# Layer 1's values and decay inputs: one set of columns in three passes of 348, 346 and 346, in place of four pieces of 512 columns and a product of its own

## The chip, the cores and the metric

The kernel runs on one core of one Trainium2 chip. The metric is the device time of one execution, in microseconds. Runs of the same kernel were repeated, and the median is given with the lowest and the highest.

## The reference

A decoder of two layers with 256 tokens and a width of 1024, in float32. Each layer has a token mixer and a gated feed-forward part with a short convolution; each of these is preceded by an RMS norm whose shift, scale and gate come from a conditioning vector (`ada`). Layer 0 mixes tokens by windowed attention. Layer 1, where the change lies, is gated linear attention with 4 heads in chunks of 64 tokens (keys of 128, values of 256 columns a head):

```python
proj = h @ w_in          # columns: q 512, k 512, v 1024, glr 16, r 1024
gk = log_sigmoid(glr @ w_gate + b_gate) / 16
# by head and chunk of 64 tokens
bcum = cumsum(gk);  blast = bcum[..., -1:, :]
q_t = q * 128**-0.5 * exp(bcum)
k_t = k * exp(-bcum)
k_d = k * exp(blast - bcum)
A = where(causal, q_t @ k_t.T, 0)
o = A @ v + q_t @ state          # state: state * exp(blast) + k_d.T @ v, chunk by chunk
# o is normed by head, gated with silu(r), and multiplied by w_out
```

The 16 columns `glr` are the input of the decay: `w_gate` is 16 x 512.

## The kernel before

Activations lie with the width on the 128 partitions (8 tiles `h[kt]`) and the 256 tokens in the columns. TensorE multiplies in float32r; to keep float32's precision, each activation and each weight is split into a high part, rounded to float32r, and a low part, the difference. A product is then three matmuls (`mm3`, lines 199 to 201): high by high, low by high, high by low. For a weight tile the load goes through SyncE's queue into `raw`, ScalarE casts it to `whi` (line 172) and VectorE subtracts to get `wlo` (line 178), each in two halves: that is `split`.

The program's instructions are ordered by a planner that estimates times while the kernel is built, with orders written by hand on top: `with behind(x)` puts what follows behind `x` on its engine without a wait of its own. `next_ada` loads 1 MB of the next conditioning weights and lets VectorE form their dot products with the conditioning vector (line 140); ScalarE turns them into `mod` (line 148).

Layer 1's mixer goes through these steps:

- Values `pv` are token-major. The stationary side of the matmul is a tile of `h` for 128 tokens, the moving side 512 of the 1024 value columns. Four loads of 1 MB (two tiles `kt` each) serve 2 x 2 x 2 products each, so 32 products, 96 matmuls of 512 columns, in four banks.
- After the second of the four, the decay: `log_gates` loads `w_glr` (120 KB), computes `glr` (16 rows by 256 tokens, 24 matmuls of 256 columns), VectorE copies it (line 1052), and `gates_of` forms `z` = `w_gate`'s 128 columns of a head by `glr`, one plain float32 product of inner size 16 for each head (line 1063).
- The gates are formed for head 0 (256 columns) and for heads 1 to 3 together (768 columns): on ScalarE `nz` = -z - b, then `ea` three times (absolute value, exponential, logarithm); on VectorE `sp`, the running sum `cs` (line 1075), `dl` (line 1079); on ScalarE the exponentials `e_d`, `e_q`, `e_k`, `dec`.
- `v` is copied out of the four banks, by ScalarE and VectorE.
- `states(hd)` for the four heads: `q` and `k` in the bank `pqk` (q of head 0 is there early), then on VectorE `k_d`, `q_t`, `k_t` (lines 1133 to 1135); TensorE turns `k_d` (`kdt`, line 1141), forms `a` (line 1152) and the state increments `kv` (line 1163); the states `st` follow on ScalarE and VectorE. `products(hd)` forms the head's output `o`, `normed_output` its norm. `gate(n)` computes `r` in the bank `pr`.
- The heads are called in the order states 0, states 1, output 0, states 2, products 1, states 3, normed output 1, products 2, gate 0 and so on. TensorE's queue fills the gaps between a head's small products with the next head's `pqk`.

Of the kernel before, what the change touches and what calls it, by code (L numbers as in the profile page):

```python
# [11 lines left out]
F32 = mybir.dt.float32  # L12
EXP_LN = "natural_log_exp_and_others"
F32R = mybir.dt.float32r
# [4 lines left out]
P = 128  # L19
# [11 lines left out]
NEG = -1e30  # L31
CONFIGS = ((128, 1), (512, 4), (2048, 16))
N_BUCKETS = 32
MAX_DISTANCE = 2048
ROWS = ((0, 512), (2, 128), (1, 128))
NROW = 768
# [21 lines left out]
def trunk(ctx: ExitStack, tc: tile.TileContext, I, out):  # L58
# [13 lines left out]
    def bank(name="ps", tag=None):  # L72
        tag = tag or next(cycle)
        return psum.tile([P, 512], F32, tag=tag, name=name, bufs={"p": 2, "s": 3, "t": 3}[tag])
# [76 lines left out]
        mod[l, piece, kt] = m  # L151
        return i, j

    def ada_chunk(l, n):
        raw = ada_load(l, n)
        for s in range(2):
            ada_dot(l, n, s, raw)


    last_load, copied, last_lo = [None], [None], [None]  # L160

    def split(src, n, dmas=1, after=((), ()), late=(), low=(), lows=True):
# [5 lines left out]
        lo = wspl.tile([P, 2048], F32R, tag="wlo", name="wlo")  # L168
        for i in range(0, n, n // 2):
            c = slice(i, i + n // 2)  # L170
            with behind(*after[i > 0]):
                copied[0] = nc.scalar.copy(hi[:, c], raw[:, c])  # L172
        if not lows:
            return hi, lo, raw, n // 2
        for i in range(0, n, n // 2):
            c = slice(i, i + n // 2)
            with behind(*(late if i else low)):
                last_lo[0] = nc.vector.tensor_tensor(lo[:, c], raw[:, c], hi[:, c].bitcast(F32), op=ALU.subtract)  # L178
        return hi, lo

    def low_part(w, i):
# [14 lines left out]
    def mm3(ps, a, b, start, stop):  # L196


        mm(ps, a[0], b[0], start=start, stop=False)  # L199
        mm(ps, a[0], b[1], start=False, stop=False)  # L200
        return mm(ps, a[1], b[0], start=False, stop=stop)  # L201
# [252 lines left out]
    shift(att, 8)  # L454
    rounds, first_loads = [0], []

    def next_ada():
        if rest:
            ada_chunk(*rest.pop(0))

    def next_half(after):
        l, n = rest[0]
# [556 lines left out]
    def gt(shape, name, dt=F32, bufs=1, tag=None):  # L1019
        return gla.tile(shape, dt, tag=tag or name, name=name, bufs=bufs)  # L1020
# [21 lines left out]

    glr_copy = []
# [11 lines left out]
    def gates_of(first, n, glr):  # L1055
        def new(name, tag, columns=n * T):
            return gt([P, columns], name, tag=f"{tag}{min(first, 1)}")

        nz = new("nz", "A")
        for i in range(n):  # L1060
            hd = first + i
            ps = bank("z", "sttt"[hd])
            mm(ps[:, :T], w_g[:, P * hd : P * hd + P], glr, start=True, stop=True)
            nc.scalar.activation(nz[:, T * i : T * i + T], ps[:, :T], AF.Identity,
                                 scale=-1.0, bias=nbg[:, hd : hd + 1])

        ea = new("ea", "B")
        nc.scalar.activation(ea, nz, AF.Abs)
# [3 lines left out]
        nc.vector.scalar_tensor_tensor(sp, nz, 0.0, ea, op0=ALU.max, op1=ALU.add)  # L1072

        cs = new("cs", "cs")
        nc.vector.tensor_tensor_scan(cs, keep[:, : n * T], sp, 0.0, op0=ALU.mult, op1=ALU.add)
        cs3 = cs.rearrange("p (n c) -> p n c", c=CH)
        last = cs3[:, :, CH - 1 : CH]
        dl = new("dl", "C")
        nc.vector.tensor_tensor(dl.rearrange("p (n c) -> p n c", c=CH), cs3,
                                last.to_broadcast([P, 4 * n, CH]), op=ALU.subtract)  # L1080
        e_d, e_q, e_k = (new(name, t) for name, t in (("e_d", "D"), ("e_q", "A"), ("e_k", "B")))
        nc.scalar.activation(e_d, dl, AF.Exp, scale=1.0 / 16)
        nc.scalar.activation(e_q, cs, AF.Exp, scale=-1.0 / 16)
        nc.scalar.activation(e_k, cs, AF.Exp, scale=1.0 / 16)
        dec = new("dec", "dec", 4 * n)
        nc.scalar.activation(dec, last.rearrange("p n c -> p (n c)"), AF.Exp, scale=-1.0 / 16)
        return e_q, e_k, e_d, dec

    pv = [[bank("pv", tg) for _ in range(2)] for tg in "ps"]
    for n in range(4):  # L1090
        with behind(*((), chain[5], chain[7], glr_copy)[n]):
            w = split(I["w_v_b"][n], 2048) if n else w_first
            if n > 1:
                next_ada()
        if n == 0:
            with behind(*chain[7]):
                whole(early_q)
        for i in range(2):
            kt = 2 * n + i
            for t in range(2):  # L1100
                ht = [y[:, P * t : P * t + P] for y in h[kt]]
                for s in range(2):
                    mm3(pv[t][s], ht, parts(w, D * i + 512 * s, 512), kt == 0, kt == KT - 1)
        if n == 1:
            gates = log_gates()
    v = [gt([P, D], f"v{t}") for t in range(2)]
    for t in range(2):
        nc.scalar.copy(v[t][:, 0:512], pv[t][0])
        nc.vector.tensor_copy(v[t][:, 512:D], pv[t][1])

    o_n = []
    last_a, last_sq, copies, kept = [None], [None], [None], [None, None]

    def states(hd):
# [23 lines left out]
        kd = gt([P, T], "kdT", bufs=2)  # L1138
        for t in range(2):
            c = slice(P * t, P * t + P)  # L1140
            nc.tensor.transpose(ps[:, c], k_d[:, c], ident)
        nc.scalar.copy(kd, ps[:, :T])

        a_t = gt([P, 2, P], "a_t", bufs=2)
# [11 lines left out]
            masked()  # L1156
        vh = slice(T * hd, T * hd + T)
        st = []
        kv = bank("kv", "t")
        for n in range(3):  # L1160
            t, r = n // 2, slice(CH * (n % 2), CH * (n % 2) + CH)
            d = (kv[:, :T], ps[:, T:], kv[:, T:])[n]
            last = mm(d, kd[r, P * t : P * t + P], v[t][r, vh], start=True, stop=True)
        if hd == 3:
            masked(last)
        for n in range(3):
# [12 lines left out]
    def output(hd, *state):  # L1179
        normed_output(hd, products(hd, *state))  # L1180

    def products(hd, q_t, a_t, st):
        po = bank("o", "s")
        for et in range(2):
            ev = slice(T * hd + P * et, T * hd + P * et + P)
            for t in range(2):
                d = po[:, T * et + P * t : T * et + P * t + P]
                mm(d, v[t][:, ev], a_t[:, t, :], start=True, stop=False)
                for n in range(2 * t, 2 * t + 2):
                    if n:  # L1190
                        last_o[0] = mm(po[:, T * et + CH * n : T * et + CH * n + CH],
                           st[n - 1][:, P * et : P * et + P], q_t[:, CH * n : CH * n + CH],
                           start=False, stop=(n % 2 == 1))
        return po

    def normed_output(hd, po, after=()):
# [99 lines left out]
def _laid_out(a):  # L1296
# [50 lines left out]
    A["w_v_b"] = wb[:, 1024:2048].reshape(4, 2, P, D).transpose(0, 2, 1, 3).reshape(4, P, 2 * D)  # L1347
    A["w_glr"] = wb[:, 2048:2064].reshape(KT, P, 16).transpose(1, 0, 2).reshape(P, KT * 16)
    A["w_glr"] = np.pad(A["w_glr"], ((0, 0), (0, P - 16)))
    A["w_r_b"] = pairs(wb[:, 2064:])  # L1350
    A["w_gate"] = a["w_gate_b"][0]
# [27 lines left out]
```

## Time and profile before

| | |
|---|---|
| median of 3 runs | 765.97 us (765.29 to 766.35) |
| the profiled execution's own time | 764.38 us |
| its span in the profile | 762.6 us |
| TensorE busy, share of the last chain | 754.2 us (99%), 94% |
| VectorE busy | 649.4 us (85%) |
| ScalarE busy | 486.2 us (64%) |
| granted TensorE clock | 1.000 |
| values, first to last product | 463.34 to 490.36 us |
| head 0's transposes start | 499.06 us |
| first product of the gate | 526.33 us |

The times of the rows are starts in the profiled execution. Its own time of 764.38 us holds 1.8 us that lie around the span, and is 1.6 us below the median of the runs.

### The profile page before, as it was taken

What the parts mean: (1) busy time and instruction counts of PE and PEld (TensorE: products, weight loads), DVE (VectorE), ACT (ScalarE), POOL (GpSimd) and SP (SyncE); (2) the same over time, 40 slices, a digit from 0 to 9 for tenths busy, and PEclk for the clock granted to TensorE, in tenths of its full rate; (3) what the DMA queues carried; (4) which work ended last, traced back from release to release, by engine and by line L of the source; (5) the groups of instructions that cost most, each with busy time, mean ns of one, the idle gap of its engine ahead of it and who ended that gap; (6) DMA issues with size and microseconds to landing.
All of it is one profiled execution on the core that took longest, in us unless ns stands there. A gap on an engine that the chain in (4) does not pass through costs nothing.

```text
span 762.6 us, 16024 instructions
## 1 busy us (share of the span) xinstructions
PE 754.2 (99%) x6394; PEld 731.5 (96%) x6394; DVE 649.4 (85%) x1185; ACT 486.2 (64%) x951; POOL 33.6 (4%) x56
## 2 busy tenths in 40 slices
PE   8999999999999999999999999999999999999997
PEld 6999999999999999999999998899999999999997
DVE  6997999898989678999999778797668999998592
ACT  6476676565566478776777456746766866666551
POOL 0001101101101010000000000000010000000100
PEclk9999999999999999999999999999999999999999
DMA  9988889778787357878556976875356777774631
GB/s 348 404 287 312 318 293 325 281 256 307 285 275 254 112 198 257 319 262 277 202 172 234 340 263 228 305 275 178 132 190 216 241 269 271 209 174 157 200 104 56
DMA packets 39225, 186.57 MB, mean 245 GB/s; under 512 B 9004, under 2 KB 11820, under 8 KB 25070
## 3 DMA queue, kind: packets, MB, share of 16 engines
q1 hardware_dynamic: 38768, 185.10, 69.6%
q8 instruction: 50, 0.82, 0.4%
q10 hardware_dynamic: 382, 0.45, 0.2%
q14 instruction: 25, 0.20, 0.1%
HBM read 184.43 MB, written 1.10 MB: 243 GB/s over the span
## 4 chain that ended last, share of the span: by engine, by line
PE 94%; DVE 3%; DMA 2%; issue 1%; ACT 0%; DVEq 0%; ACTq 0%
PE pab L199 10%; PE pab L200 10%; PE pab L201 10%; PE pqk L199 5%; PE pd L199 5%; PE pd L200 5%; PE pd L201 5%; PE pqk L201 5%; PE pqk L200 5%; PE pv L199 3%; PE pv L200 3%; PE pv L201 3%; PE pqk L675 2%; PE py L199 2%; PE py L201 2%; PE py L200 2%
## 5 line engine op out<-in xcount | busy, mean ns | idle before, releaser
L172 ACT CAST whi<-raw 128x1024 fp32r<-128x1024 f32 (+4 forms) x262 | 237.7, 951 | 92.6 <-PE pab L200 35.5
L178 DVE TENSOR_TENSOR wlo<-raw,whi 128x1024 fp32r<-128x1024 f32 (+3 forms) x246 | 263.8, 1097 | 38.5 <-ACT whi L172 37.5
L200 PE MATMUL pab<-hlo,whi 128*128 128x256 f32 x672 | 184.6, 276 | 0.0
L201 PE MATMUL pab<-hhi,wlo 128*128 128x256 f32 x672 | 184.6, 276 | 0.0
L199 PE MATMUL pab<-hhi,whi 128*128 128x256 f32 x672 | 183.2, 277 | 0.0
L200 PEld LDWEIGHTS pab<-hlo,whi 128*128 128x128 f32 x672 | 126.0, 188 | 0.2
L201 PEld LDWEIGHTS pab<-hhi,wlo 128*128 128x128 f32 x672 | 126.1, 188 | 0.0
L199 PEld LDWEIGHTS pab<-hhi,whi 128*128 128x128 f32 x672 | 125.1, 188 | 0.1
L140 DVE CUSTOM_DVE_ANT_0 ada_raw<-ada_raw,c_bc 128x1024 f32<-128x1024 f32 x96 | 114.1, 1229 | 4.7 <-DMA ada_raw<-in_w_ada 4.7
L199 PE MATMUL pqk<-hhi,whi 128*128 128x256 f32 x356 | 98.0, 281 | 0.0
L200 PE MATMUL pqk<-hlo,whi 128*128 128x256 f32 x356 | 97.4, 279 | 0.0
L201 PE MATMUL pqk<-hhi,wlo 128*128 128x256 f32 x356 | 96.8, 279 | 0.2 <-DVE wlo L178 0.2
L200 PE MATMUL pd<-glo,whi 128*128 128x256 f32 x308 | 84.8, 276 | 0.0
L201 PE MATMUL pd<-ghi,wlo 128*128 128x256 f32 x308 | 84.8, 276 | 0.0
L199 PE MATMUL pd<-ghi,whi 128*128 128x256 f32 x308 | 84.7, 276 | 0.0
L201 PEld LDWEIGHTS pqk<-hhi,wlo 128*128 128x128 f32 x356 | 65.9, 188 | 1.1 <-issue 0.7
L200 PEld LDWEIGHTS pqk<-hlo,whi 128*128 128x128 f32 x356 | 66.7, 188 | 0.1
L199 PEld LDWEIGHTS pqk<-hhi,whi 128*128 128x128 f32 x356 | 66.5, 188 | 0.1
L200 PEld LDWEIGHTS pd<-glo,whi 128*128 128x128 f32 x308 | 57.7, 188 | 0.0
L201 PEld LDWEIGHTS pd<-ghi,wlo 128*128 128x128 f32 x308 | 57.7, 188 | 0.0
L199 PEld LDWEIGHTS pd<-ghi,whi 128*128 128x128 f32 x308 | 57.7, 188 | 0.0
L962 ACT ACTIVATE r<-pab,small 128x256 f32<-128x256 f32 x86 | 47.5, 561 | 7.0 <-DVE r L965 6.7
(269 smaller groups left out, 1498.8 us busy)
## 6 DMA issues: line engine op xcount, KB each, us to landing
raw<-in_w_up SPq DMA_DIRECT2D x42, 1024.0 KB, 4.9
ada_raw<-in_w_ada SPq DMA_DIRECT2D x29, 1024.0 KB, 5.8
raw<-in_w_down SPq DMA_DIRECT2D x28, 704.0 KB, 4.3
ada_raw<-in_w_ada SPq DMA_DIRECT2D x38, 512.0 KB, 6.8
raw<-in_wqk SPq DMA_DIRECT2D x18, 1024.0 KB, 6.9
raw<-in_wv SPq DMA_DIRECT2D x14, 768.0 KB, 6.5
raw<-in_w SPq DMA_DIRECT2D x7, 960.0 KB, 6.5
raw<-in_w_out_a SPq DMA_DIRECT2D x4, 1024.0 KB, 6.9
```

The costliest lines, as they stand in the source:

```text
L140: i = nc.vector.tensor_tensor_reduce(w, w, c_bc, op0=ALU.mult, op1=ALU.add, scale=1.0, scalar=0.0, accum_out=dot,)
L172: copied[0] = nc.scalar.copy(hi[:, c], raw[:, c])
L178: last_lo[0] = nc.vector.tensor_tensor(lo[:, c], raw[:, c], hi[:, c].bitcast(F32), op=ALU.subtract)
L199: mm(ps, a[0], b[0], start=start, stop=False)
L200: mm(ps, a[0], b[1], start=False, stop=False)
L201: return mm(ps, a[1], b[0], start=False, stop=stop)
L675: mm(pqk[i], w[a], h[kt][b], start=s and i % 2 == 0 and (a, b) == (0, 0), stop=e and i % 2 == 1 and b == 1)
L962: nc.scalar.activation(r, u[:, :T], AF.Identity, scale=cw[2], bias=col(C_CB + 44 * l + f))
```

## The change

The 16 decay inputs become columns of the same product as the values: 16 + 1024 = 1040 columns, in three passes of 348, 346 and 346. The first pass holds the 16 and value columns 0 to 331, the others 346 value columns each. The weights lie in memory padded to 384 columns a pass and tile, in six loads of 768 KB (pass by half of the tiles `kt`), which `split` casts and subtracts through a view of the used columns. A pass uses two banks, one for each half of the tokens, so that there are 144 matmuls of 348 or 346 columns. The passes' halves are ordered: pass 0 first half, pass 1 first half, pass 0 second half, pass 1 second half, pass 2.

The decay inputs thus come out with the tokens on the partitions. `stack_parts` splits them there into a high and a low part and lays high, low and high again at columns 0, 32 and 64 of a zeroed 128 x 128 tile for each half of the tokens (six small VectorE instructions). `turn_parts` turns the two tiles with two transposes into one bank, and VectorE copies it as `glr`, now 128 x 256 float32r. `w_gate` lies in memory as 128 x 512 with its 16 rows at 0, 32 and 64; ScalarE casts it and VectorE puts the low part at rows 64 to 79. So one float32r product of inner size 128 a head gives high by high, low by high and high by low at once. The transposes come after the first two of the four tiles of pass 1's second half, z after its last.

Besides, `next_ada` takes an order, and for head 3 `products(1)` is formed before head 3's state increments, its second half behind head 3's transposes.

```diff
-        w_first = split(I["w_v_b"][0], 2048, late=last_x[1:])
+        w_first = [columns(0, 0, late=last_x[:1]), columns(1, 0, low=last_x[1:], late=last_x[1:])]
...
+    def columns(n, half, **order):
+        c = (348, 346, 346)[n]
+        return split(I["w_v_b"][n, half], 4 * 384, view=lambda w: w.rearrange("p (k c) -> p k c", k=2)[:, :, 0:c], **order)
...
-    w_g = gt([16, 512], "w_g")
-    nc.sync.dma_start(w_g, I["w_gate"])
+    w_g = gt([P, 512], "w_g", F32R)
+    w_raw = gt([P, 512], "w_raw", tag="C1")
+    nc.sync.dma_start(w_raw, I["w_gate"])
+    with behind(*chain[7]):
+        nc.scalar.copy(w_g, w_raw)
+        own = slice(STACKED[2], STACKED[2] + 16)
+        nc.vector.tensor_tensor(w_g[own, :], w_raw[own, :], w_g[own, :].bitcast(F32), op=ALU.subtract)
+    stacked = gt([P, 2, P], "stacked", F32R)
+    nc.gpsimd.memset(stacked.bitcast(F32), 0.0)
...
+    def stack_parts(pv):
+        for t in range(2):
+            hi, lo, again = (stacked[:, t, at : at + 16] for at in STACKED)
+            ps = pv[t][:, 0:16]
+            nc.vector.tensor_copy(hi, ps)
+            nc.vector.tensor_tensor(lo, ps, hi.bitcast(F32), op=ALU.subtract)
+            nc.vector.tensor_copy(again, hi.bitcast(F32))
+
+    def turn_parts():
+        ps = bank("glr", "t")
+        for t in range(2):
+            last = nc.tensor.transpose(ps[:, P * t : P * t + P], stacked[:, t, :].bitcast(F32), ident)
+        low_rank.append(nc.vector.tensor_copy(glr, ps[:, 0:T]))
+        return last
 
     def log_gates():
-        with behind(*chain[5]):
-            w_gl = split(I["w_glr"], 7 * 16 + P)
-        ps = bank("glr", "t")
-        for kt in range(KT):
-            mm3(ps[:, :T], parts(w_gl, 16 * kt), h[kt], kt == 0, kt == KT - 1)
-        glr = gt([16, T], "glr")
-        glr_copy.append(nc.vector.tensor_copy(glr, ps[:16, :T]))
-        return [gates_of(*part, glr) for part in PARTS]
+        for tg in "st":
+            ps = bank("z", tg)
+            for i in range(2):
+                hd = len(sums_of)
+                sums_of.append(ps[:, T * i : T * i + T])
+                last = mm(sums_of[hd], w_g[:, P * hd : P * hd + P], glr, start=True, stop=True)
+        return last
...
-    for n in range(4):
-        with behind(*((), chain[5], chain[7], glr_copy)[n]):
-            w = split(I["w_v_b"][n], 2048) if n else w_first
-            if n > 1:
-                next_ada()
...
+    def values(n, half, w, kts=range(4), after=()):
+        c = (348, 346, 346)[n]
+        for j in kts:
+            kt = 4 * half + j
+            with behind(*after):
+                for t in range(2):
+                    ht = [y[:, P * t : P * t + P] for y in h[kt]]
+                    last = mm3(pv[n][t][:, 0:c], ht, parts(w, 384 * j, c), kt == 0, kt == KT - 1)
+        return last
...
+    values(0, 0, w_first[0])
+    last = values(1, 0, w_first[1])
+    with behind(*chain[3]):
+        w = columns(0, 1)
+    last = values(0, 1, w, after=[last])
+    with behind(*chain[7]):
+        whole(early_q)
+    stack_parts(pv[0])
+    with behind(*chain[7]):
+        w = columns(1, 1)
+        next_ada(last_lo[0])
+    last = values(1, 1, w, range(2), [last])
+    with behind(last):
+        last = turn_parts()
+    keep_values(0)
+    last = values(1, 1, w, range(2, 4), [last])
+    with behind(last):
+        last = log_gates()
+    pv.append([bank("pv", "t") for _ in range(2)])
+    gates = [gates_of(*part) for part in PARTS]
+    with behind(*low_rank):
+        w = columns(2, 0)
+        next_ada(last_lo[0])
+    keep_values(1)
+    last = values(2, 0, w, after=[last])
+    w = columns(2, 1)
+    values(2, 1, w, after=[last])
+    keep_values(2)
...
-    po1 = products(1, *s1)
-    s3 = states(3)
-    normed_output(1, po1, last_a)
+    po1 = []
+
+    def ahead(turned):
+        po1.append(products(1, *s1, last=turned))
+        return last_o
+
+    s3 = states(3, ahead)
+    normed_output(1, po1[0], last_a)
```

More of the change, by code (lines that the diff above doesn't have):

```diff
@@ L152, in ada_dot, with ada_chunk, split @@
         return i, j
-    def ada_chunk(l, n):
+    def ada_chunk(l, n, *after):
         raw = ada_load(l, n)
-        for s in range(2):
-            ada_dot(l, n, s, raw)
+        with behind(*after):
+            for s in range(2):
+                ada_dot(l, n, s, raw)
     last_load, copied, last_lo = [None], [None], [None]
-    def split(src, n, dmas=1, after=((), ()), late=(), low=(), lows=True):
+    def split(src, n, dmas=1, after=((), ()), late=(), low=(), lows=True, view=None):
         raw = wraw.tile([P, 2048], F32, tag="raw", name="raw")
@@ L168, in split @@
         lo = wspl.tile([P, 2048], F32R, tag="wlo", name="wlo")
+        part = view or (lambda w: w)
         for i in range(0, n, n // 2):
@@ L171, in split @@
             with behind(*after[i > 0]):
-                copied[0] = nc.scalar.copy(hi[:, c], raw[:, c])
+                copied[0] = nc.scalar.copy(part(hi[:, c]), part(raw[:, c]))
         if not lows:
@@ L177, in split @@
             with behind(*(late if i else low)):
-                last_lo[0] = nc.vector.tensor_tensor(lo[:, c], raw[:, c], hi[:, c].bitcast(F32), op=ALU.subtract)
+                last_lo[0] = nc.vector.tensor_tensor(part(lo[:, c]), part(raw[:, c]), part(hi[:, c].bitcast(F32)), op=ALU.subtract)
         return hi, lo
@@ L455, in trunk, with next_ada @@
     rounds, first_loads = [0], []
-    def next_ada():
+    def next_ada(*after):
         if rest:
-            ada_chunk(*rest.pop(0))
+            ada_chunk(*rest.pop(0), *after)
     def next_half(after):
@@ L1089, in trunk @@
     pv = [[bank("pv", tg) for _ in range(2)] for tg in "ps"]
-    for n in range(4):
-        with behind(*((), chain[5], chain[7], glr_copy)[n]):
-            w = split(I["w_v_b"][n], 2048) if n else w_first
-            if n > 1:
-                next_ada()
[L1095 to L1105, printed above, removed]
@@ L1106, in trunk @@
-    v = [gt([P, D], f"v{t}") for t in range(2)]
-    for t in range(2):
-        nc.scalar.copy(v[t][:, 0:512], pv[t][0])
-        nc.vector.tensor_copy(v[t][:, 512:D], pv[t][1])
+    v = [gt([P, D], f"v{t}") for t in range(2)]
+    def values(n, half, w, kts=range(4), after=()):
+        c = (348, 346, 346)[n]
+        for j in kts:
+            kt = 4 * half + j
+            with behind(*after):
+                for t in range(2):
+                    ht = [y[:, P * t : P * t + P] for y in h[kt]]
+                    last = mm3(pv[n][t][:, 0:c], ht, parts(w, 384 * j, c), kt == 0, kt == KT - 1)
+        return last
@@ new lines, in keep_values @@
+    def keep_values(n):
+        first, c = VCUTS[n]
+        at = 0 if n else 16
+        for t, copy in enumerate((nc.scalar.copy, nc.vector.tensor_copy)):
+            copy(v[t][:, first : first + c], pv[n][t][:, at : at + c])
+    values(0, 0, w_first[0])
[9 more added lines that the diff above has]
+        next_ada(last_lo[0])
@@ L1111, in trunk, with states @@
+    keep_values(2)
     o_n = []
     last_a, last_sq, copies, kept = [None], [None], [None], [None, None]
-    def states(hd):
+    def states(hd, between=lambda turned: ()):
         if hd == 0:
@@ L1140, in states @@
             c = slice(P * t, P * t + P)
-            nc.tensor.transpose(ps[:, c], k_d[:, c], ident)
+            last_kd = nc.tensor.transpose(ps[:, c], k_d[:, c], ident)
         nc.scalar.copy(kd, ps[:, :T])
@@ L1158, in states @@
         st = []
+        ahead = between(last_kd)
         kv = bank("kv", "t")
@@ L1162, in states @@
             d = (kv[:, :T], ps[:, T:], kv[:, T:])[n]
-            last = mm(d, kd[r, P * t : P * t + P], v[t][r, vh], start=True, stop=True)
+            with behind(*ahead):
+                last = mm(d, kd[r, P * t : P * t + P], v[t][r, vh], start=True, stop=True)
         if hd == 3:
@@ L1180, in output, with products @@
         normed_output(hd, products(hd, *state))
-    def products(hd, q_t, a_t, st):
+    def products(hd, q_t, a_t, st, last=None):
         po = bank("o", "s")
@@ L1185, in products @@
             ev = slice(T * hd + P * et, T * hd + P * et + P)
[L1186 to L1193, printed above, removed]
+            with behind(*([last] if last and et else [])):
+                for t in range(2):
+                    d = po[:, T * et + P * t : T * et + P * t + P]
+                    mm(d, v[t][:, ev], a_t[:, t, :], start=True, stop=False)
+                    for n in range(2 * t, 2 * t + 2):
+                        if n:
+                            last_o[0] = mm(po[:, T * et + CH * n : T * et + CH * n + CH],
+                               st[n - 1][:, P * et : P * et + P], q_t[:, CH * n : CH * n + CH],
+                               start=False, stop=(n % 2 == 1))
         return po
```

24 lines of the change are left out of this document (15 added, 9 removed).

## The prediction, on record before the changed kernel ran

> **What bounds the kernel now.** I read the page's list of engines and the chain that ended last first, then the stretches of layer 1's mixer.
>
> ```profile
> PE 754.2 (99%) x6394; PEld 731.5 (96%) x6394; DVE 649.4 (85%) x1185; ACT 486.2 (64%) x951; POOL 33.6 (4%) x56
> PE 94%; DVE 3%; DMA 2%; issue 1%; ACT 0%; DVEq 0%; ACTq 0%
> ```
> ```profile
> core 0: us, PE busy (x) PEld busy (x) DVE busy (x) ACT busy (x) POOL busy (x), PEclk, DMA share, GB/s
> 464.00:482.00 18.00, 18.00 (x91) 15.25 (x90) 16.41 (x29) 11.62 (x24) 0.00 (x0) 1.00 0.78 300
> 485.00:499.00 14.00, 14.00 (x98) 12.96 (x97) 12.20 (x16) 13.01 (x22) 0.00 (x0) 1.00 0.68 239
> 526.00:562.00 36.00, 36.00 (x316) 35.89 (x315) 24.75 (x40) 25.34 (x42) 0.00 (x0) 1.00 0.51 176
> 757.00:760.00 3.00, 0.32 (x3) 0.08 (x1) 1.30 (x4) 1.19 (x3) 0.00 (x0) 1.00 0.10 38
> 760.00:762.60 2.60, 0.00 (x0) 0.00 (x0) 0.00 (x0) 0.00 (x0) 0.00 (x0) 0.90 0.41 158
> ```
>
> TensorE works 99% of the span and is 94% of the last chain. In the stage that is changed (464 to 499) it never stops, and after it, from 526 to 562, it is busy 36.00 us of 36.00. So a microsecond of TensorE work taken out here reaches the end, unless TensorE then comes to something that isn't ready. VectorE and ScalarE are the candidates: from 485 to 499 they are busy 12.20 and 13.01 of 14.00 us.
>
> **TensorE's work, part by part.** Matmuls are pipelined, so I price them by the distance of their starts.
>
> ```profile
> 463.34 0.59 PE L199 MATMUL pv<-whi,hhi 128*128 128x512 f32 x1
> 474.85 0.28 PE L201 MATMUL glr<-hhi,wlo 128*128 128x256 f32 x1
> 477.32 0.28 PE L201 MATMUL glr<-hhi,wlo 128*128 128x256 f32 x1
> 482.26 0.40 PE L199 MATMUL pv<-whi,hhi 128*128 128x512 f32 x1
> 484.85 0.40 PE L201 MATMUL pv<-whi,hlo 128*128 128x512 f32 x1
> 490.36 0.39 PE L201 MATMUL pv<-whi,hlo 128*128 128x512 f32 x1
> 499.06 0.38 PE L1141 MATMUL kdt<-ident,k_d 128*128 128x128 f32 x2
> 505.77 0.28 PE L201 MATMUL pqk<-hhi,wlo 128*128 128x256 f32 x1
> 506.22 0.60 PE L1152 MATMUL a<-q_t,k_t 128*128 128x128 f32 x4
> ```
>
> From 484.85 to the values' last product at 490.36 lie 8 further products of three passes each, 24 steps: 0.2294 us for 512 columns. The third and the last of glr's 24 products are 2.47 us apart, 21 steps: 0.1177 for 256 columns. Straight between the two, 346 columns take 0.1177 + 90 x 0.000436 = 0.157 (by the 512 row's price per column 0.155, by the 256 row's 0.159).
> - Values and decay inputs: 96 x 0.2294 = 22.02 becomes 144 x 0.157 = 22.61: **+0.6** (+0.3 to +0.9).
> - glr's 24 own products go: 24 x 0.1177 = **-2.82**.
> - z: from 482.26 to 484.85 there are 2.59 us, which hold two value steps and z's four products of K=16, eight passes: 2.59 - 2 x 0.2294 = **-2.13**. The four float32r products that take their place, as wide as glr's: 4 x 0.1177 = **+0.47**.
> - Two transposes of the stacked parts, 128x128 in float32 like head 1's between 505.77 and 506.22: 0.45 less two float32r steps, **+0.2**.
>
> The sum is -3.68: TensorE would come to head 0's transposes (`kdt`, 499.06 before) at 495.4.
>
> **Is k_d of head 0 there by then?** The transposes wait for VectorE's k_d, and the other heads' products stand behind them on TensorE. Rows of the two engines on the way:
>
> ```profile
> 483.32 0.91 ACT L1064 ACTIVATE nz<-z,nbg 128x256 f32<-128x256 f32 x2 [0.29 <-PE z L1063]
> 484.13 0.41 ACT L1068 ACTIVATE ea<-nz 128x256 f32<-128x256 f32 x1
> 485.45 2.00 ACT L172 CAST whi<-raw 128x1024 fp32r<-128x1024 f32 x2
> 487.34 0.85 ACT L1068 ACTIVATE ea<-nz 128x768 f32<-128x768 f32 x1
> ```
> ```profile
> 486.54 2.36 DVE L178 TENSOR_TENSOR wlo<-raw,whi 128x1024 fp32r<-128x1024 f32 x2 [2.72 <-ACT whi L172]
> 488.81 0.42 DVE L1072 SCALAR_TENSOR_TENSOR sp<-nz,ea 128x256 f32<-128x256 f32 x1
> 489.41 0.69 DVE L1109 COPY v<-pv 128x512 f32<-128x512 f32 x1 [0.17 <-PE pv L201]
> 490.01 0.68 DVE L1075 TENSOR_TENSOR_SCAN cs<-keep,sp 128x256 f32<-128x256 f32 x1
> 491.72 0.95 DVE L1072 SCALAR_TENSOR_TENSOR sp<-nz,ea 128x768 f32<-128x768 f32 x1
> 492.59 1.22 DVE L178 TENSOR_TENSOR wlo<-raw,whi 128x1024 fp32r<-128x1024 f32 x1
> 493.73 1.75 DVE L1075 TENSOR_TENSOR_SCAN cs<-keep,sp 128x768 f32<-128x768 f32 x1
> 495.39 1.20 DVE L178 TENSOR_TENSOR wlo<-raw,whi 128x1024 fp32r<-128x1024 f32 x1
> 496.51 0.42 DVE L1134 SCALAR_TENSOR_TENSOR q_t<-early_q,e_q 128x256 f32<-128x256 f32 x1
> 496.85 0.42 DVE L1133 TENSOR_TENSOR k_d<-pqk,e_d 128x256 f32<-128x256 f32 x1
> 497.51 0.95 DVE L1079 TENSOR_TENSOR dl<-cs 128x768 f32<-128x768 f32 x1
> ```
>
> Before, k_d ended at 497.27, 1.8 us ahead of its use. The order of instructions of the changed build puts, between z and k_d:
> - z ends after 96 of the 144 value products: 463.34 + 96 x 0.157 + 0.2 = 478.6; with the product's own latency (rows of 0.28 to 0.39) and four steps of 0.12, `nz` starts at about 479.1. If casts of the last pass still stand ahead on ScalarE, 480.
> - ScalarE then runs four `nz` (0.81 for two, 483.32 to 484.13: 1.6), two `ea` of 256 and two of 768 columns (a step is the duration less some 0.1 of overlap: 2 x 0.31 + 2 x 0.75), two small `mod` and a small copy (an estimate of 0.6), and the first half of head 1's weight cast (1.0). That is 5.3 us: 484.4 (to 485.4). All of these stand ahead of that cast, which before went in at 485.45, behind three of the `nz` and two `ea`.
> - VectorE waits for that cast, then runs: two halves of `wlo` 2.27; sp of head 0 0.34; half of `v` of pass 1 0.43 (between 0.60 for 512 columns and 0.33 for 256); sp of the other heads 0.87; cs 0.60; `wlo` 1.14; their cs 1.66; `wlo` 1.12; dl 0.33 (as k_d's kind); two `wlo` 2.27; their dl 0.87; q_t 0.34; k_d 0.42. Sum 12.66. Against before, two more `wlo` halves (2.3) and the wide dl (0.9), which stood behind k_d at 497.51, now stand ahead of it.
>
> So k_d ends at 497.1 to 498.1 and the transposes start 0.2 later; I take 497.8. TensorE, there at 495.4, stands idle for some 2.4 us (2.0 to 2.9), where before it had no wait. Of the 3.7 us, **1.2** are left (0.8 to 1.7).
>
> **Behind that.** `products(1)` goes ahead of head 3's state products, its second half behind head 3's transposes. That is no work more or less, but one more place where TensorE turns from float32r to float32 products between head 0's transposes and the gate (nine for eight). Between 505.77 and 506.22 three steps and two transposes are already 0.2 over the float32r pace; a turn costs 0.1 to 0.2. VectorE, late now, can also hold back head 1's k_d by some tenths. I take **+0.5** for both (+0.2 to +0.9; below nothing too, to -0.2, if a wait inside head 3 is covered by the moved products).
>
> Edits that I cost at nothing: the loads are six of 768 KB where four of 1 MB and 120 KB went, +0.4 MB, with the DMA share at 0.78 and TensorE never waiting for a load in this stretch; the cover is the pass ahead, and it is gone if a load comes over 4 us later. The strided form of the split (two runs of 346) is bounded by these rows, the second with a strided output, to 0.02 us each, twelve in all on each engine:
>
> ```profile
> L621 DVE COPY v<-pv x7: 405/409/409, 69.2 to 248.4; 64x256 f32<-64x256 f32 x7
> L622 DVE COPY v<-pv x7: 427/428/428, 69.6 to 248.8; 64x256 f32<-64x256 f32 x7
> ```
>
> The six 16-column copies that stack the parts have no row; they lie between a tiny instruction and a k_d (0.1 to 0.42 each, 0.6 to 2.5 in all) and run while twelve value products of pass 1 (1.9 us) cover them.
>
> **Sum:** -3.68 + 2.4 (the wait) + 0.5 = **-0.7** us, with -1.3 to +0.9 for the ends. The profiled execution of before took 764.38 us, 1.6 below the median of the runs, 765.97; set against the median the forecast is **765.3** (this case's own range 764.7 to 766.9). About 0.2%, 1.5 us, is what a measurement of this kernel can tell from no change.
>
> **Rivals.**
> 1. *The gain is kept.* k_d is there when TensorE comes. For it: VectorE stood idle 2.72 us ahead of 486.54, so it has room that a better meeting with ScalarE's casts could use; and the durations I sum are from a stretch with both engines full. Against it: the order is fixed, and 12.66 us behind a cast that ends at 484.4 leave over 2 us to find. The whole gain is -3.7 + 0.5 = -3.2, 762.8; half of the wait gone gives -1.9, 764.1.
> 2. *TensorE's clock drops in the new wait (slower).* It decides if a wait of 2.0 to 2.9 us is long enough. Price: at the kernel's start, after an idle 2.24 us, float32 products of 512 columns took 0.94 each, later ones 0.52:
>
> ```profile
> 2.24 3.75 PE L123 MATMUL cb<-c_row,ones_d 1*128 1x512 f32 x4 [2.24 <-DMA c_row<-in_c]
> 11.26 1.03 PE L405 MATMUL rows<-oh,tab 33*16 33x512 f32 x2
> ```
>
>    So 3.75 us or more at about half speed: at least 1.9 us lost, up to 3.5 if it lasts twice as long; -0.7 + 1.9 = +1.2 to +2.8, middle 768.0. Against it: at the end of the span TensorE did almost nothing from 757.00 on and the clock is still 1.00 up to 760, so an idle of nearly 3 us left it whole. [...]
> 3. *The stacked copies come late (slower).* They stand behind two `ada` dots and two weight subtracts on VectorE:
>
> ```profile
> L140 DVE CUSTOM_DVE_ANT_0 ada_raw<-ada_raw,c_bc 128x1024 f32<-128x1024 f32 x96 | 114.1, 1229 | 4.7 <-DMA ada_raw<-in_w_ada 4.7
> 463.72 0.33 SPq L133 DMA_DIRECT2D ada_raw<-in_w_ada  x1
> ada_raw<-in_w_ada SPq DMA_DIRECT2D x29, 1024.0 KB, 5.8
> ```
>
>    An `ada` load issued at 463.72 lands at about 469.5, and the dots have to start by about 472, since pass 0 is complete after 72 value products (474.7) and its turned parts are due after 84 (476.5). If the load slips by more than 2.5 us, the two dots (2.46) fall between pass 0's end and the copies; transposes, z, ScalarE's chain and k_d all come later by up to 2.4: +1.7, 767.7. Against it: 4.7 us in 96 dots is all that dots waited for their loads in the whole span.
>
> **How the numbers follow.** The forecast 0.45 (765.3), the gain kept wholly or by more than half 0.35 (the sum on VectorE carries the verdict, and it hangs on where two full engines meet), the clock 0.10 (768.0), the late copies 0.10 (767.7). Faster by over 0.2% needs below 764.4: rival 1 nearly whole, with a little of the forecast's lower end, 0.36. Slower needs over 767.5: rivals 2 and 3 and nothing of the forecast, 0.19 with a little of both falling inside. The rest is 0.45. The range reaches to the kept gain's far end, 762.8, but for its last part, and to the slower cases' middle: 762.9 to 767.9.
>
> **What would show it.** Right: TensorE idle for 2 to 3 us ahead of head 0's `kdt`, released by VectorE's k_d; `kdt` at 497 to 498.5; value steps of 0.155 to 0.159; the granted clock 1.00 throughout. Rival 1: no such idle, `kdt` near 495.5. Rival 2: idle and then products of twice the step. Rival 3: TensorE idle ahead of the transposes into `glr`, or z after 480. The forecast is wrong at its root if the value products take over 0.165 each, or if idle time appears after 526.

## The result, and the profile after

The changed kernel takes 766.38 us (median of 22 runs, 765.16 to 769.34), the kernel before 765.03 us (22 runs, 763.92 to 766.35). The ratio is 1.0021, 95% interval 1.0013 to 1.0029: slower by 0.21%, where 0.7 us less was forecast. The profiled execution took 768.63 us, 2.3 above its kernel's median; before, it was 1.6 below what was then the median. Two page lines of the changed kernel, busy time by engine and the last chain, and then its span with the mean granted clock:

```profile
PE 755.3 (98%) x6416; PEld 736.3 (96%) x6416; DVE 651.0 (85%) x1195; ACT 486.5 (63%) x955; POOL 33.0 (4%) x57
PE 90%; DVE 5%; DMA 2%; ACT 2%; issue 1%; DVEq 0%; ACTq 0%
```
```profile
core 0: 766.8 us, clock 0.996
```

TensorE's part of the last chain fell from 94% to 90%, VectorE's rose from 3% to 5%, ScalarE's from 0 to 2%. The mean granted clock was 1.000 before. So something made TensorE wait, and something took its clock. Its list of waits (total us, times, longest us), which before had none over 0.3 us behind the kernel's start:

```profile
PE cb L125 <- DMA c_row<-in_c: 3.0, 1, 3.0
PE kdt L1195 <- DVE k_d L1187: 3.0, 1, 3.0
```

The place in time, in TensorE's timeline (start us, us, operation, and in brackets the wait ahead of it):

```profile
466.28 0.51 PE L203 MATMUL pv<-whi,hhi 128*128 128x348 f32 x1
475.05 0.33 PE L203 MATMUL pv<-whi,hhi 128*128 128x348 f32 x1
477.75 0.32 PE L205 MATMUL pv<-whi,hlo 128*128 128x348 f32 x1
481.93 0.64 PE L1082 MATMUL z<-glr,w_g 128*128 128x256 f32 x4
498.09 0.28 PE L205 MATMUL pqk<-hhi,wlo 128*128 128x256 f32 x1
501.35 0.69 PE L1195 MATMUL kdt<-ident,k_d 128*128 128x128 f32 x2 [2.98 <-DVE k_d L1187]
503.34 0.41 PE L203 MATMUL pqk<-hhi,whi 128*128 128x256 f32 x1
503.55 0.41 PE L204 MATMUL pqk<-hlo,whi 128*128 128x256 f32 x1
505.11 0.28 PE L205 MATMUL pqk<-hhi,wlo 128*128 128x256 f32 x1
505.23 0.28 PE L203 MATMUL pqk<-hhi,whi 128*128 128x256 f32 x1
530.23 0.36 PE L203 MATMUL pr<-hhi,whi 128*128 128x256 f32 x1
```

TensorE's last product ahead of head 0's transposes ends at 498.37, and the transposes start at 501.35. Behind that wait float32r products of 256 columns are 0.21 us apart (503.34, 503.55); two microseconds later, the same products are 0.12 apart again (505.11, 505.23). The granted clock by stretches of half a microsecond (the columns are those of the windows shown with the prediction) says why:

```profile
498.50:499.00 0.50, 0.00 (x0) 0.00 (x0) 0.50 (x2) 0.50 (x1) 0.00 (x0) 1.00 0.42 98
500.50:501.00 0.50, 0.00 (x0) 0.00 (x0) 0.50 (x3) 0.28 (x1) 0.00 (x0) 0.98 0.98 410
501.00:501.50 0.50, 0.15 (x1) 0.15 (x2) 0.50 (x2) 0.50 (x1) 0.00 (x0) 0.50 1.02 410
503.50:504.00 0.50, 0.50 (x5) 0.50 (x4) 0.50 (x3) 0.05 (x1) 0.00 (x0) 0.50 0.67 279
504.00:504.50 0.50, 0.50 (x4) 0.50 (x4) 0.50 (x1) 0.33 (x1) 0.00 (x0) 0.61 0.05 16
504.50:505.00 0.50, 0.50 (x7) 0.50 (x6) 0.50 (x2) 0.00 (x0) 0.00 (x0) 1.00 0.97 131
```

The clock falls to 0.50 at 501.0, 2.6 us after TensorE's last product, and is back at 504.4: 3.4 us at half speed. This is rival 2 of the prediction, in its place and near its price. Of the 22 runs, 20 have a mean clock of 0.994 to 0.996 and two 0.998; of the 73 runs of before that stand beside the experiments below, none is under 0.998. (A mean of 0.998 or 0.999 can come from the idle time at the span's end alone: in the changed kernel's profile the clock stands at 0.50 from 763.8 to the end at 766.8, and these 3.0 us by themselves make a mean of 0.998; it falls there in before too, in the prediction's row from 760 to 762.6.)

One thing in this profile isn't the change's doing. Its stage starts 2.94 us later than before's (466.28 against 463.34), and that comes from the first 20 us: the first input landed at 3.0 us instead of 2.2, and six float32 products there took 2.74 us instead of 1.47, at about half speed. (The column of the granted clock reads 1.00 there; that the clock was slower is my estimate from the products' times.) Both differ between the profiles of kernels whose edits lie inside the stage: kd_first below has 2.2 and 2.74 us, dl_behind 3.0 and 1.53. So I compare distances inside the stage, from the first value product (`pv`) to the gate's first (`pr`): before 526.33 - 463.34 = 62.99 us, after 530.23 - 466.28 = 63.95. The change costs 0.96 us there, by rows that do not hold the start.

### The profile page after: what moved, and what is told of

It reads as the page before. It is cut to its first block, busy times and chain, and to the rows that moved or that the text cites. A ratio compares the mean times of both kernels' runs of the same rounds, so it can differ in the third digit from the quotient of the medians.

```text
span 766.8 us, 16084 instructions
## 1 busy us (share of the span) xinstructions
PE 755.3 (98%) x6416; PEld 736.3 (96%) x6416; DVE 651.0 (85%) x1195; ACT 486.5 (63%) x955; POOL 33.0 (4%) x57
## 4 chain that ended last, share of the span: by engine, by line
PE 90%; DVE 5%; DMA 2%; ACT 2%; issue 1%; DVEq 0%; ACTq 0%
PE pab L204 10%; PE pab L203 10%; PE pab L205 10%; PE pqk L203 6%; PE pqk L205 6%; PE pqk L204 6%; PE pd L204 4%; PE pd L203 4%; PE pd L205 4%; PE pv L203 3%; PE pv L204 3%; PE pv L205 3%; PE pqk L679 2%; PE py L203 2%; PE py L205 2%; PE py L204 2%
## 5 line engine op out<-in xcount | busy, mean ns | idle before, releaser
L182 DVE TENSOR_TENSOR wlo<-raw,whi 128x1024 fp32r<-128x1024 f32 (+5 forms) x248 | 264.3, 1091 | 32.2 <-ACT whi L176 31.4
L203 PE MATMUL pv<-whi,hhi 128*128 128x384 f32 (+2 forms) x160 | 53.2, 338 | 0.0
```

Of the source, the lines that this page charges most:

```text
L182: last_lo[0] = nc.vector.tensor_tensor(part(lo[:, c]), part(raw[:, c]), part(hi[:, c].bitcast(F32)), op=ALU.subtract)
```

## The experiments

All edits are to the changed kernel. "Stage" is the distance from the first value product to the gate's first product in the run's profile, "turn" that from the first value product to head 0's transposes. Times are medians.

| kernel | us | before, run beside it | ratio, 95% interval | turn | stage |
|---|---|---|---|---|---|
| before | | | | 35.72 | 62.99 |
| changed | 766.38 | 765.03 | 1.0021 (1.0013 to 1.0029) | 35.07 | 63.95 |
| filled_wait | 765.89 | 765.07 | 1.0014 (1.0002 to 1.0026) | 34.93 | 62.38 |
| kd_first | 763.82 | 765.07 | 0.9982 (0.9972 to 0.9993) | 32.26 | 61.02 |
| kd_first_ed | 764.53 | 765.07 | 0.9993 (0.9974 to 1.0013) | 32.46 | 64.52 |
| dl_behind | 763.87 | 765.07 | 0.9985 (0.9971 to 1.0000) | 34.05 | 61.03 |
| dl_behind_filled | 763.76 | 764.58 | 0.9988 (0.9977 to 1.0000) | 34.41 | 61.40 |
| dl_behind_old_order | 763.55, one run | 764.58 | | 34.18 | 61.18 |
| kd_first_ada_late | 768.50 | 764.58 | 1.0045 (1.0029 to 1.0060) | 32.04 | 66.62 |
| kd_first_ada_last | 764.77 | 764.75 | 0.9992 (0.9979 to 1.0005) | 32.39 | 60.15 |
| kd_first_ada_last2 | 764.90 | 764.75 | 1.0003 (0.9987 to 1.0019) | 32.17 | 59.92 |

**filled_wait: the same wait, filled with work.** It parts the wait from the clock. The diff shows the filling alone; the edit also forms head 1's `pqk` earlier in the program, so that the filling can stand behind its last product, and the planner then placed some products of heads 2 and 3 otherwise behind the transposes.

```diff
+            for _ in range(22):
+                with behind(*filled):
+                    filled = [mm(ps[:, 0:T], h[0][0][:, 0:P], h[1][0], start=True, stop=True)]
             for t in range(2):
                 c = slice(P * t, P * t + P)
-                last_kd = nc.tensor.transpose(ps[:, c], k_d[:, c], ident)
+                with behind(*filled):
+                    last_kd = nc.tensor.transpose(ps[:, c], k_d[:, c], ident)
```

> The changed kernel with 22 float32r products of 256 columns more on TensorE, into the bank of head 0's transposes and of no use, issued between head 1's last pqk product and those transposes; all else as in the changed kernel. They fill the wait of 2.98 us with work (22 x 0.113 = 2.5 us). Theory (the wait's idle time drops the granted clock to 0.50 from 501.0 to 504.4, and that costs about 1.5 us on top of the wait): the transposes start at the same distance from the stage's begin, the clock stays 1.00 there, and the time is 1.5 us below the changed kernel, 764.9, level with before. Rival (the slow clock costs nothing, because VectorE sets the pace behind the wait): no change from the changed kernel, 766.4, though the clock is 1.00.

TensorE's timeline of this kernel, and its windows:

```profile
464.14 0.51 PE L203 MATMUL pv<-whi,hhi 128*128 128x348 f32 x1
496.07 2.80 PE L1205 MATMUL kdt<-hhi 128*128 128x256 f32 x22
499.07 0.44 PE L1209 MATMUL kdt<-ident,k_d 128*128 128x128 f32 x2 [0.20 <-DVE k_d L1189]
526.52 0.36 PE L203 MATMUL pr<-hhi,whi 128*128 128x256 f32 x1
```
```profile
498.00:501.00 3.00, 2.80 (x24) 2.46 (x23) 3.00 (x7) 1.67 (x4) 0.00 (x0) 1.00 1.02 412
501.00:504.00 3.00, 3.00 (x24) 2.49 (x23) 3.00 (x7) 0.80 (x3) 0.00 (x0) 1.00 0.62 178
```

The transposes come where they came (34.93 against 35.07 us from the stage's begin), the clock stays 1.00, and from the transposes to the gate it takes 526.52 - 499.07 = 27.45 us instead of 530.23 - 501.35 = 28.88. So the slow clock costs about 1.43 us, and useless work in the place of the wait saves them. As the order behind the transposes is not quite the same, I set a second reading beside it: in the changed kernel TensorE worked from 501.35 to 504.4 at half speed, and half of these 3.05 us is 1.5. The rival, that VectorE sets the pace there anyway, falls in the stage. All twelve runs have a mean clock of 0.998 or more. But the median, 765.89, lies between the theory's 764.9 and the rival's 766.4, nearer the rival: it moved by 0.5 us instead of 1.5, the intervals of the two ratios overlap, and the kernel stays 0.14% slower than before. This profile lost some 2 us later, in the feed-forward part, with a wait of 1.4 us for `sqacc`. The clock's price is shown by the stage, not by the whole time.

**kd_first: VectorE's order.** The wide `dl` and head 3's two weight subtracts go behind head 0's `k_t`. (`head0` is the instruction that forms head 0's `k_t`; the second half of `gates_of` is called later.)

```diff
-        nc.vector.tensor_tensor(dl.rearrange("p (n c) -> p n c", c=CH), cs3,
-                                last.to_broadcast([P, 4 * n, CH]), op=ALU.subtract)
+        with behind(*head0):
+            nc.vector.tensor_tensor(dl.rearrange("p (n c) -> p n c", c=CH), cs3,
+                                    last.to_broadcast([P, 4 * n, CH]), op=ALU.subtract)
...
-            w = split(I["w_qk_b"][hd], 2048)
+            w = split(I["w_qk_b"][hd], 2048, **({}, {}, {}, dict(low=head0, late=head0))[hd])
```

> The changed kernel with one edit in the order of VectorE: the wide dl of heads 1 to 3 and the two weight subtracts of head 3 go behind head 0's q_t, k_d and k_t, as far as they stood behind k_d or near it before. Theory (VectorE's order alone makes the wait, and the wait makes the clock drop): the 3.1 us leave the way to k_d, of which ScalarE's e_d, which comes at 497.7 to 498.1 in any case, takes some back; the wait falls from 2.98 to 0.3 to 0.9 us, the clock stays, and the time is 766.4 - 2.3 - 1.5 = 762.6, up to 763.9 if heads 1 to 3 wait for what was moved. Rival 1 (the clock costs nothing): 764.1 to 765.4. Rival 2 (TensorE's new work is dearer than its rows say, so there is no gain to free): no better than before, 765.0.

TensorE's waits, and the transposes:

```profile
PE kv L1228 <- ACT kdT L1205: 0.7, 1, 0.7
PE kdt L1204 <- DVE k_d L1194: 0.2, 1, 0.2
```
```profile
497.87 0.33 PE L1204 MATMUL kdt<-ident,k_d 128*128 128x128 f32 x1 [0.17 <-DVE k_d L1194]
```

The wait went from 2.98 to 0.17 us and the stage from 63.95 to 61.02. The time is 763.82, in the upper part of what was expected, and with 0.9982 (0.9972 to 0.9993) it is below both kernels. So TensorE's saving was real, and VectorE's order had hidden it. Not all of it is kept: from the transposes to the gate it takes 28.76 us where filled_wait takes 27.45. Of that, 0.7 is a new wait of TensorE for ScalarE's copy of a later head; the cause of the other 0.6 is open.

**kd_first_ed** also puts ScalarE's casts of head 3's weights behind head 0's `e_d` (`first_ed` is that instruction).

```diff
-dict(low=head0, late=head0)
+dict(after=(first_ed, first_ed), low=head0, late=head0)
```

> As kd_first, and on ScalarE the two weight casts of head 3 go behind head 0's e_d, so that e_d does not stand behind them. Theory: head 0's transposes do not wait at all, and the whole of TensorE's saving is kept but for small waits in heads 1 to 3: 0.3 to 0.7 us less than kd_first, 762.0 to 763.2. Rival (e_d was not what k_d waited for): the same as kd_first.

The waits of TensorE, ScalarE's timeline at the longest of them, and the windows behind it:

```profile
PE kv L1230 <- ACT kdT L1207: 2.8, 1, 2.8
PE kdt L1206 <- DVE k_d L1196: 0.4, 1, 0.4
```
```profile
515.23 0.29 ACT L152 ACTIVATE mod<-dot,small 128x1 f32<-128x1 f32 x1 [4.31 <-DVE dot L142]
516.38 0.39 ACT L150 ACTIVATE mod<-dot,one_b,small 128x1 f32<-128x1 f32 x1 [0.63 <-DVE dot L142]
517.15 0.36 ACT L1207 COPY kdT<-kdt 128x256 f32<-128x256 f32 x1
```
```profile
517.00:518.00 1.00, 0.44 (x4) 0.42 (x5) 1.00 (x4) 0.51 (x2) 0.00 (x0) 1.00 0.53 98
519.00:520.00 1.00, 1.00 (x4) 0.91 (x5) 0.56 (x2) 0.68 (x2) 0.00 (x0) 0.50 1.00 426
```

The expectation failed, and so did its rival. The transposes of head 0 still waited 0.4 us, and a wait of 2.8 came up at a later head: ScalarE's copy of the turned `k_d` stands behind two `mod` instructions that wait for VectorE's `ada` dots. Here too the clock is at 0.50 behind the wait. So the same pair, a wait of nearly 3 us and a slow clock, came up at another place. This profile is of a run with a mean clock of 0.997. Four of the twelve runs are of that kind (0.993 to 0.997, 766.4 to 768.6 us); the median of the eight others is 763.1, which is inside what was expected. What those eight waited for, no profile shows.

**dl_behind: only the wide `dl` is moved**, a smaller dose of the same wait.

```diff
-        nc.vector.tensor_tensor(dl.rearrange("p (n c) -> p n c", c=CH), cs3,
-                                last.to_broadcast([P, 4 * n, CH]), op=ALU.subtract)
+        with behind(*head0):
+            nc.vector.tensor_tensor(dl.rearrange("p (n c) -> p n c", c=CH), cs3,
+                                    last.to_broadcast([P, 4 * n, CH]), op=ALU.subtract)
```

> The changed kernel with only the wide dl (0.87 us) behind head 0's k_t. The wait falls from 2.98 to about 2.1 us. It tells how long an idle time drops the clock. [...] If the clock costs nothing: 765.5.

TensorE's longest wait, and the windows that hold its second half and its end:

```profile
PE kdt L1204 <- DVE k_d L1194: 2.0, 1, 2.0
```
```profile
496.00:497.00 1.00, 0.01 (x1) 0.02 (x1) 1.00 (x4) 0.00 (x0) 0.00 (x0) 1.00 1.01 426
497.00:498.00 1.00, 1.00 (x8) 0.87 (x9) 1.00 (x2) 0.37 (x1) 0.00 (x0) 1.00 1.09 418
```

An instruction of 0.87 us that gets out of the way takes 1.0 us from the wait and, in this profile, the slow clock with it; the stage falls by 2.9 us, to 61.03, as far as with kd_first. (Wait and clock make 2.4 of it; the other 0.5 lies between the transposes and the gate, 26.98 us here and 27.45 in filled_wait, and its cause is open.) The ten runs are of two kinds: five with a mean clock of 0.998 or 0.999 and a median of 763.0, five with 0.996 or 0.997 and 764.9.

**dl_behind_filled** fills that wait as filled_wait does, with 18 products.

> dl_behind with 18 float32r products of no use on TensorE in its wait of 2.0 us. In dl_behind half of the runs had a mean clock of 0.998 or 0.999 and a median of 763.0, the others 0.996 or 0.997 and 764.9. Theory (in the second kind the clock drops in the wait): with the wait filled no run is under 0.998, and the median is that of the first kind, about 763.0, where that of all dl_behind runs was 763.9. Rival (the second kind has its drop elsewhere, or runs differ for another reason): both kinds stay, and the median stays at 763.9.

None of the twelve runs has a clock under 0.998, as the theory wanted. The median did not follow: 763.76 instead of 763.0, a ratio of 0.9988 against 0.9985 of dl_behind. That the low clocks come from this wait is shown by five of ten runs against none of twelve; but no profile shows one of the five, and what they cost in the time of dl_behind is open.

**dl_behind_old_order** undoes the new place of `products(1)`.

```diff
-    po1 = []
-    def ahead(turned):
-        po1.append(products(1, *s1, last=turned))
-        return last_o
-    s3 = states(3, ahead)
+    po1 = products(1, *s1)
+    s3 = states(3)
```

> dl_behind without the change's new place for products(1): it is formed ahead of states(3) again, as in the kernel before. What that part of the change is worth by itself, by the distance from the values' first product to the gate's first (dl_behind 61.03): if the moved products fill a wait inside head 3, it grows by 0.3 to 1.3; if they only add a turn between kinds of products, it shrinks by 0.1 to 0.3.

The stage is 61.18 us against 61.03, neither of the two sizes expected, and the wait ahead of it is 0.14 longer (2.10 against 1.96). From the transposes to the gate both take 27.0 us. So this part of the change is worth nothing that shows.

**kd_first_ada_late, kd_first_ada_last and kd_first_ada_last2** look for the rest of the saving. The first puts the third `ada` piece behind head 3's `k_t`, the second behind the last head's norm, both on top of kd_first_ed; the third does it on top of kd_first. The diff shows the new place of the second and third.

```diff
-    for _ in range(3):
+    for _ in range(2):
         next_ada()
...
     normed_output(3, po3)
+    for _ in range(1):
+        next_ada(last_on[0])
```

> kd_first_ed with one more edit in the order of VectorE: the third of the three next ada pieces that VectorE forms beside heads 1 to 3 goes behind head 3's k_t. In kd_first_ed ScalarE's copy of head 2's turned k_d stood behind a mod that waits for those dots, TensorE waited 2.8 us for it, and the clock fell behind that wait. Theory (that was the only reason why kd_first_ed was no better than kd_first): no wait over 0.5 us in the stage, from the values' first product to the gate's first 59.3 to 60.3 us (before 62.98, the changed kernel 63.95, kd_first 61.02), and 762.0 to 763.0. Rival (VectorE sets the pace of heads 1 to 3 in any case): another wait takes its place, 61.0 or more, and 764.

> kd_first_ed with the third next ada piece of that stretch behind the last head's norm on VectorE (in kd_first_ada_late it stood ahead of the sum for a head's norm, and TensorE waited 4.2 us for that). Theory: no wait over 0.5 us from the values' first product to the gate's first, 59.3 to 60.3 us, as was expected of kd_first_ada_late up to that wait; 762.0 to 763.0 against 764.6 for before. Rival (VectorE has no room for that piece anywhere near): a wait takes its place again, 61 or more, and 764 or more.

> kd_first with the third next ada piece behind the last head's norm, ScalarE's casts left where kd_first has them. It parts the two edits of kd_first_ada_last: head 0's transposes wait 0.2 to 0.7 us for ScalarE's e_d, as in kd_first, and nothing behind waits: 59.7 to 60.7 us to the gate's first product, 762.3 to 763.3. Rival as for kd_first_ada_last.

The waits of TensorE, of the first and of the second:

```profile
PE ms L215 <- DVE oacc L1269: 4.2, 1, 4.2
```
```profile
PE py L203 <- ACT r L1296: 1.1, 1, 1.1
PE py L203 <- ACT whi L176: 0.9, 1, 0.9
PE kdt L1206 <- DVE k_d L1196: 0.3, 1, 0.3
```

In kd_first_ada_late the dots stood ahead of the sum for a head's norm: a wait of 4.2 us, and 768.50. The profiled run's mean clock is 0.992 over a span of 767.5 us; if it was 1.00 or 0.50 throughout, that is, by an estimate from these two numbers, some 12 us at half speed, the span's end included. The other two reach what was expected of the stage, 60.15 and 59.92 us, three microseconds below before, and are still no faster than before over the whole: two waits of 1.1 and 0.9 us for ScalarE come up in the output projection `py` behind the stage. The rival holds for the whole time, but not for that reason alone: both profiles are of runs with a mean clock of 0.999, while four of twelve runs of each kernel have 0.996 or 0.997, with medians of 765.9 and 767.0 us. The medians of the eight others are 763.75 and 764.15, against 764.75 for before. Where the clock falls in the four, no profile shows. kd_first, with only VectorE's order changed, has the lowest ratio of all, though those of dl_behind and dl_behind_filled lie inside its interval.

## Why the prediction was wrong

**Right: TensorE's own work.** The values' steps measure (477.75 - 475.05) / 17 = 0.159 us, where 0.157 was taken and 0.159 was the upper end. TensorE would have come to the transposes at 35.07 - 2.98 = 32.09 us from the stage's begin, against 35.72 before: -3.63, forecast -3.68. kd_first shows the same without the wait (32.26, of which 0.17 is waited). That the two agree to 0.05 us is in part luck: the values at 0.159 cost 0.3 more than taken, and the 72 products of `pqk` behind them cost 0.3 less, which nobody forecast. Their step is (498.09 - 490.95) / 63 = 0.113 us in the changed kernel and (498.94 - 490.58) / 71 = 0.118 before; why is open.

**Right in kind, too small: the wait.** It was put where it came, for the reason given, at 2.4 us (2.0 to 2.9); it was 2.98. VectorE's chain from head 1's subtracts to the end of k_d took 12.63 us (488.66 to 501.29), forecast 12.66. What was late was its start, and the rows of ScalarE and VectorE show why:

```profile
480.61 1.44 ACT L176 CAST whi<-raw 128x692 fp32r<-128x692 f32 x2 [1.05 <-DMA raw<-in_w_v_b]
482.45 1.14 ACT L176 CAST whi<-raw 128x512 fp32r<-128x512 f32 x2
483.50 1.56 ACT L1092 ACTIVATE nz<-z,nbg 128x256 f32<-128x256 f32 x4
487.58 1.99 ACT L176 CAST whi<-raw 128x1024 fp32r<-128x1024 f32 x2
```
```profile
488.66 2.36 DVE L182 TENSOR_TENSOR wlo<-raw,whi 128x1024 fp32r<-128x1024 f32 x2 [0.92 <-ACT whi L176]
497.40 2.35 DVE L182 TENSOR_TENSOR wlo<-raw,whi 128x1024 fp32r<-128x1024 f32 x2
499.67 0.95 DVE L1107 TENSOR_TENSOR dl<-cs 128x768 f32<-128x768 f32 x1
500.87 0.42 DVE L1187 TENSOR_TENSOR k_d<-pqk,e_d 128x256 f32<-128x256 f32 x1
```

`nz` was expected at 479.1 on before's clock of times, 480 with casts ahead of it; less the 2.94 us of the later start it came at 480.56. Of that, 0.4 is z itself (481.93 - 2.94 = 478.99, where 478.6 was taken). The rest is ScalarE's: a load of the values' weights kept it idle for 1.05 us, and two casts of 0.5 us each, of head 0's k weights, stood behind the casts of that load and still ahead of `nz`. `nz` starts 483.50 - 466.28 = 17.22 us from the stage's begin. The loads had been costed at nothing because TensorE never waited for one; here ScalarE did, and TensorE in the end through it. That is read from the rows; no run moved the load.

**Wrong: the clock.** The sum took the wait at its length alone and put nothing on the clock behind it. In the stage, this is the step that turned the sign: without the 1.43 us the sum below is -0.47. (Over the whole time the sign is not shown to hang on it, since filled_wait stays above before; it turns when the wait goes too, in kd_first.) Rival 2 had the place right and the price somewhat high (at least 1.9, measured 1.43 by filled_wait), but was given a chance of 0.10, because the clock stood at 1.00 up to 760 at the end of before's span with TensorE nearly idle from 757. That row doesn't bear the argument: it tells how long that idle time could last at that point, not how short a wait can be and still be too long. At before's end the clock fell at 762.1, 4.7 us after TensorE's last product; in the changed kernel 2.6 us without a product were enough.

The slow stretch lasts 3.4 us in this profile, from 501.0 to 504.4, and TensorE had not been idle for as long ahead of it: the 3.4 us before 501.0 hold 0.8 us of products (497.6 to 498.37). No run shows that a wait of 2.4 us costs nothing beyond its length, as the forecast's sum has it: behind 2.98 us the clock stood at 0.50, and with 1.96 us, in dl_behind, five of ten runs had a mean clock of 0.996 or 0.997.

**The sum, by the measured terms:** -3.63 + 2.98 (the wait) + 1.43 (the clock) + 0.18 (the rest from the transposes to the gate, 28.88 - 27.27 - 1.43; forecast 0.5) = +0.96 us, the stage's difference. The medians differ by 1.35; the remaining 0.4 has no place in these traces. The forecast's own sum was also added up loosely: -3.68 + 2.4 + 0.5 is -0.78, not -0.7, and what it leaves of the gain (0.8 to 1.7) with the 0.2 to 0.9 behind it ends at -1.5 and +0.1, not at -1.3 and +0.9. By its own terms, then, a slower kernel was hardly in it: the term that was missing is the clock.

**Rivals 1 and 3.** The gain was not kept, though kd_first shows that it could be. The `ada` dots did hold the stacked copies up a little (pass 0's last product ends at 478.07, the copies run from 478.65 to 479.28), but not far enough for TensorE to notice: the transposes into `glr` followed at 479.81 with twelve value products still ahead of z, and z came where TensorE's own work puts it, 15.65 us from the stage's begin.

## What to carry to other kernels

When work is taken from the engine that bounds a kernel, add up what it will meet sooner, instruction by instruction in the order of the build, and start that sum from the latest load on the way, not only from the last matrix product. A wait of TensorE can have a second price: here the wait of 2.98 us cost about 1.43 us more, since the clock stood at 0.50 for 3.4 us behind it, and with a wait of 1.96 us five of ten runs had a lower mean clock and five had not. Before giving up a change that frees TensorE, look at what the newly critical engine does ahead of the one instruction that TensorE waits for, and move it behind that instruction: here that turned +0.21% into -0.18%. And look at the clock of every run, not only of the one that was profiled: two kernels whose profiled runs had a mean clock of 0.999 (kd_first_ada_last and kd_first_ada_last2) had four runs of twelve each with a lower one, 0.996 or 0.997, and a longer time.

## What the runs showed of the hardware

In the changed kernel's profile the granted clock fell to 0.50 after 2.6 us without a product (498.37 to 501.0), with 0.8 us of products in the 3.4 us before the fall, and stayed there for 3.4 us although TensorE worked again from 501.35. In dl_behind's profile a wait of 1.96 us left it at 1.00, while five of its ten runs had a lower mean clock (0.996 or 0.997), and none of twelve had once the wait was filled. So with a wait of about 2 us the mean clock was lower in some executions of one kernel and not in others.

The fall does not have to come during the wait: in kd_first_ed TensorE started again at 517.56 after 2.8 us, and the clock fell at 518.4. Nor does 3.4 us fit every profile. In kd_first_ada_late, with its wait of 4.2 us, the gate's first product, at 529.40, took 0.56 us where it took 0.36 in the changed kernel, and the mean clock of 0.992 over 767.5 us makes, by the estimate above, some 12 us at half speed; of the changed kernel's span, 3.4 us behind the wait and 3.0 at the end were at 0.50. Why it was so much is open.
